# Row vectors of an attention kernel made by a VectorE block transpose and short transfers instead of TensorE transposes

## The chip, the cores and the metric

The kernel runs on one core of a Trainium2 chip. The metric is device time in microseconds (us) of one execution. Each time is the median of several executions, and the profile is one further execution with every instruction recorded. The engines are TensorE (PE), VectorE (DVE), ScalarE (ACT) and GpSimd (POOL); DMA transfers are issued from queues in order, here the queue of SyncE (SP) for nearly all, and POOL's for the loads of K, Q and V.

## The reference, cut to what matters

Two layers of a mixer trunk over 256 context tokens and 2048 latent tokens, width 1024, all in float32. Latent queries attend over all 2304 keys, context queries over the 256 context keys. The change touches only the softmax and the product of its result with a gate:

```python
def attend(q, k, v):                        # 8 heads, 96 wide, values 64 wide
    def one_block(qi):
        s = jnp.einsum('bqhd,bkhd->bhqk', qi, k).astype(jnp.float32) * sm_scale
        p = jax.nn.softmax(s, axis=-1).astype(v.dtype)
        return jnp.einsum('bhqk,bkhd->bqhd', p, v)
    ...
y_a = attn * jax.nn.silu(g_a)               # then two convolution branches y_b, y_c
y = jnp.concatenate([y_a, y_b, y_c], axis=-1)
x_new = x + gate[:, None, :] * (y @ w_out[l])
```

## The kernel before, in words

Activations are kept transposed, features on the partitions and tokens along the row. Products that need float32 accuracy are split into a rounded high part and a low rest and done as three matmuls (`mm3`, lines 194 to 196). Each layer has four phases, one after the other with some overlap: tokens (normalised input), features (the wide product with W_in, and the convolutions, whose vector work is the `cc` and `sgcl` lines), attention, project (the product with W_out). All instructions are emitted into a scheduler that lists them by priority, so the order on an engine follows from dependences, priorities and rotating buffers, not from a hand-written list.

**Attention.** A job is one head and one block of 512 queries: 32 jobs a layer, and in layer 0 eight more of 256 context queries, one for each head (these are grouped with the fourth block of their head). A job does two things.

- Max pass (`prepare`). For each 128 queries and each 512 keys, one matmul `pmax` (L985) and one VectorE reduction (L986), 20 of each for a job; only two PSUM buffers hold `pmax`. `finish` (L989) makes the negated maximum of every query, one column of 128 for each query tile. `turn` makes that column a row: up to four matmuls `pmt` (L994) against an identity, and one ScalarE copy (L995) into row 96 of the query tile Q. K has ones there, so that the score matmul subtracts the maximum by itself. The max pass of a later job runs `LEAD` pairs of key tiles ahead of the present one, at a raised priority.
- Key loop. For each of nine pairs of key tiles: six score matmuls (L1073 to 1075; the first reads 97 rows, the row of maxima among them), four ScalarE exponentials giving p and ph (L1076, 1077), one GpSimd subtraction pl = p - ph (L1078), two VectorE additions into the running sum `acc` in PSUM (L1083 for the first, L1085), and four matmuls into `po` with the values (L1100, 1101). `close` stores `o` to DRAM (`o_d`, L1108), transposes the sums (`psum_t`, L1113), adds them up and takes reciprocals into `rinv` (L1116), one number for each query and head.

**Project.** `prepare_y` builds blocks of y for 512 tokens. For the four attention blocks (k below 4, two heads each) it loads the two halves of the attention result (`yr`, `ylo`, from `o_d`, L1168 and 1169) and the gate (`yg`, L1170). It then spreads the reciprocals: for each of four token tiles a ScalarE copy to 64 columns for each head (`rr`, L1174) and a TensorE transpose into PSUM (`prr`, L1175). Three VectorE products follow: r + lo (L1176), times `prr` (L1177), times the gate (L1178). Blocks of y are prepared while the last jobs of attention still run. The output is stored from the SP queue (`out_xT`, L1202).

Of the kernel before, what the change touches and what calls it, by code (L numbers as in the profile page):

```python
# [9 lines left out]
F32 = mybir.dt.float32  # L10
F32R = mybir.dt.float32r
I32 = mybir.dt.int32
AF = mybir.ActivationFunctionType
ALU = mybir.AluOpType
AX = mybir.AxisListType
# [3 lines left out]
P = 128  # L19
# [4 lines left out]
NT = SEQ + CTX  # L24
NTT = NT // P
DEPTH = 2
H = 8
# [24 lines left out]
NE = 2  # L52
# [11 lines left out]
RR = 3  # L64
# [20 lines left out]
def trunk(ctx: ExitStack, tc: tile.TileContext, ins, out):  # L85
    nc = tc.nc
    V, S, G, PE = nc.vector, nc.scalar, nc.gpsimd, nc.tensor
# [4 lines left out]
    cst = pool(ctx, "cst")  # L92
    ps = pool(ctx, "ps", space=PSUM)
    dr = pool(ctx, "dr", space=DRAM)

    def psum(tag, name):
        return ps.tile([P, 512], F32, tag=tag, name=name, bufs={"a": 3, "b": 2}.get(tag, 1))
# [39 lines left out]
    gain = [cst.tile([P, KD, 2], F32, name=f"gain{l}") for l in range(DEPTH)]  # L137

    rcol = rinv[1][:, :, 0:1]
    mx = [cst.tile([P, 4, 97], F32R, name=f"mx{i}") for i in range(2)]  # L140
    zero = rinv[0].rearrange("p t h -> p (t h)")[:, :97]
    G.memset(zero, 0.0)
    for t in mx:
        for i in range(4):
            G.tensor_copy(t[:, i], zero)

# [8 lines left out]
    x1_d = dr.tile([D, NT], F32, name="x1_d")  # L157
    xs = [ins["xT"], x1_d]
    xg_d = dr.tile([D, NT], F32, name="xg_d")

    def rsqrt_steps(y, v, tmp, tmi):

# [30 lines left out]
    def mm3(out_, ahi, alo, bhi, blo, first, last):  # L193
        PE.matmul(out_, lhsT=ahi, rhs=bhi, start=first, stop=False)  # L194
        PE.matmul(out_, lhsT=ahi, rhs=blo, start=False, stop=False)  # L195
        PE.matmul(out_, lhsT=alo, rhs=bhi, start=False, stop=last)  # L196


    def halves(l, j, ws, hi, lo, by=None):
# [739 lines left out]
    def attention(l, start):  # L939
# [17 lines left out]
        count = [0]  # L957
# [12 lines left out]
        def prepare(h, s, n, k0):  # L970

            K, Vt, Q = kv[h]
            keys = [(a, min(512, NT - a)) for a in range(k0 * P, NT, 512)]
            m = mx[count[0] % 2]

            early = count[0] < NE
            count[0] += 1

            part = m
            nq = n // P  # L980
            steps = []

            def chunk(t, c, a, w):
                pm = psum("b", "pmax")
                PE.matmul(pm[:, :w], lhsT=Q[0:QK, s // P + t, 0], rhs=K[0:QK, a // P : (a + w) // P, 0], start=True, stop=True)  # L985
                V.tensor_reduce(part[:, t, c : c + 1], pm[:, :w], axis=AX.X, op=ALU.max)  # L986

            def finish():
                V.tensor_reduce(m[:, 0:nq, 96:97], part[:, 0:nq, 0 : len(keys)], axis=AX.X, op=ALU.max, negate=True)  # L989

            def turn():
                px = psum("b" if early else "e", "pmt")
                for t in range(nq):
                    PE.matmul(px[0:97, t * P : (t + 1) * P], lhsT=m[:, t, :], rhs=idr, start=True, stop=True)  # L994
                S.copy(Q[96:97, s // P : (s + n) // P, 0], px[96:97, :n].rearrange("p (a t) -> p a t", t=P))  # L995

            for t in range(nq):
                for c, (a, w) in enumerate(keys):
                    steps.append(lambda t=t, c=c, a=a, w=w: chunk(t, c, a, w))
            return steps, finish, turn  # L1000

        LEAD = 3
        queue = []
        sums = [0]

# [45 lines left out]
        for idx, job in enumerate(jobs):  # L1053
            h = job[0][0]
            if job[0][1] == (1024 if h else 512) and h + 1 < H:
                load(h + 1)
            pairs = [(j, it) for j in job for it in range(j[3], NTT, 2)]
            for pi, ((h, s, n, k0), kt0) in enumerate(pairs):
                if idx == len(jobs) - 1 and pi == len(pairs) - AE:
                    mark = tc.cur_priority  # L1060
                K, Vt, Q = kv[h]
                first, final = kt0 == k0, kt0 == NTT - 2
                if first:
                    po = psum("c", "po")
                    acc = psum("d", "acc")
                p = tp.tile([P, 2, 512], F32, tag="p", name="p", bufs=4)
                ph = tp.tile([P, 2, 512], F32R, tag="ph", name="ph", bufs=3)
                pl = tp.tile([P, 2, 512], F32R, tag="pl", name="pl", bufs=3)
                scs = []
                for z in range(2):  # L1070
                    kt, qt = kt0 + z, slice(s // P, (s + n) // P)
                    sc = psum("a", "sc")
                    PE.matmul(sc[:, :n], lhsT=K[0:97, kt, 0], rhs=Q[0:97, qt, 0], start=True, stop=False)  # L1073
                    PE.matmul(sc[:, :n], lhsT=K[0:QK, kt, 0], rhs=Q[0:QK, qt, 1], start=False, stop=False)  # L1074
                    PE.matmul(sc[:, :n], lhsT=K[0:QK, kt, 1], rhs=Q[0:QK, qt, 0], start=False, stop=True)  # L1075
                    S.activation(p[:, z, :n], sc[:, :n], AF.Exp, scale=scale)  # L1076
                    S.activation(ph[:, z, :n], sc[:, :n], AF.Exp, scale=scale)  # L1077
                G.tensor_tensor(pl[:, :, :n], p[:, :, :n], ph[:, :, :n].bitcast(F32), op=ALU.subtract)  # L1078
                flush()

                for z in range(2):
                    if first and z == 0:
                        V.tensor_copy(acc[:, :n], p[:, 0, :n])  # L1083
                    else:
                        V.tensor_tensor(acc[:, :n], acc[:, :n], p[:, z, :n], op=ALU.add)  # L1085
                for z in range(2):
                    at = pi + (z + 1) / 2 + LEAD
                    if at <= len(pairs):
                        ahead(idx + 1, at / len(pairs))
                    else:  # L1090
                        ahead(idx + 1, 1)
                        ahead(idx + 2, (at - len(pairs)) / len(pairs))
                if pi == len(pairs) // 2:
                    split_mods()
                if pi == len(pairs) - ME:
                    use_mods()

                def products(kt0=kt0, n=n, Vt=Vt, ph=ph, pl=pl, po=po, first=first, final=final):
                    for z in range(2):
                        PE.matmul(po[:, :n], lhsT=Vt[:, kt0 + z, :], rhs=ph[:, z, :n], start=first and z == 0, stop=False)  # L1100
                        PE.matmul(po[:, :n], lhsT=Vt[:, kt0 + z, :], rhs=pl[:, z, :n], start=False, stop=final and z == 1)  # L1101

                def close(h=h, s=s, n=n, po=po, acc=acc):
                    accs = op.tile([P, 512], F32, tag="o", name="accs", bufs=3)
                    S.activation(accs[:, :n], acc[:, :n], AF.Copy, scale=2.0)
                    o = op.tile([P, 512], F32, tag="o", name="o", bufs=3)
                    S.copy(o[:, :n], po[:, :n])
                    nc.sync.dma_start(o_d[l][h, :, s : s + n], o[:, :n])  # L1108

                    nq = n // P  # L1110
                    px = psum("e", "psum_t")
                    for t in range(nq):
                        PE.transpose(out=px[:, t * P : (t + 1) * P], in_=accs[:, t * P : (t + 1) * P], identity=idn)  # L1113
                    sm = tp.tile([P, 4], F32, tag="sm", name="sm", bufs=2)
                    V.tensor_reduce(sm[:, :nq], px[:, :n].rearrange("p (t k) -> p t k", k=P), axis=AX.X, op=ALU.add)
                    V.reciprocal(rinv[l][:, s // P : s // P + nq, h], sm[:, :nq])  # L1116

                late.append(products)
                if final:
                    late.append(close)  # L1120
# [10 lines left out]
    def project(l, start):  # L1131
# [22 lines left out]
        def prepare_y(bi):  # L1154
# [5 lines left out]
            for k in order:  # L1160
# [3 lines left out]
                else:  # L1164
# [3 lines left out]
                        nc.sync.dma_start(r[64 * z : 64 * z + 64, :n], o_d[l][2 * k + z, 0:64, s : s + n])  # L1168
                        nc.sync.dma_start(lo[64 * z : 64 * z + 64, :n], o_d[l][2 * k + z, 64:128, s : s + n])
                    nc.sync.dma_start(g[:, :n], sga_d[l][k * P : (k + 1) * P, s : s + n])  # L1170
                    px = psum("b" if bi == 0 else "cde"[k % 3], "prr")
                    for t in range(n // P):
                        rr = rp.tile([P, 2, 64], F32, tag="rr", name="rr", bufs=RR)
                        S.copy(rr, rinv[l][:, s // P + t, 2 * k : 2 * k + 2].unsqueeze(2).to_broadcast([P, 2, 64]))  # L1174
                        PE.transpose(out=px[:, t * P : (t + 1) * P], in_=rr.rearrange("p a b -> p (a b)"), identity=idn)  # L1175
                    V.tensor_tensor(r[:, :n], r[:, :n], lo[:, :n], op=ALU.add)  # L1176
                    V.tensor_tensor(r[:, :n], px[:, :n], r[:, :n], op=ALU.mult)  # L1177
                    V.tensor_tensor(r[:, :n], r[:, :n], g[:, :n], op=ALU.mult)  # L1178
                split(yh[:, k, :n], yl[:, k, :n], r[:, :n], V if bi == 0 and (SPV & 4 and k < 4 or SPV & 8 and k >= 4) else None)
                yield  # L1180

# [128 lines left out]
```

## Time and profile before

| what | us |
|---|---|
| median of 3 runs | 3695.61 (3680.32 to 3699.47) |
| the profiled execution's own time | 3695.0 |
| its span, from first to last instruction | 3693.2 |
| PE busy | 3529.8 (96%) |
| DVE busy | 2888.8 (78%) |
| POOL busy | 2341.6 (63%) |
| ACT busy | 2166.7 (59%) |

The mean granted clock of TensorE is 0.978 of full speed. Matmuls overlap in the trace: each is listed with the time from its start to its modelled end, while the next one may start earlier, so that what a matmul costs in a full row is the distance between starts. A profile group names the line, the engine, the output and the inputs of an operation.

### The profile page before, as it was taken

To read this page: it belongs to the slowest core of one execution; us is meant where nothing else is said; L and a number is where in the kernel's file an instruction comes from. 1 tells how busy PE (TensorE), PEld (TensorE's weight loads), DVE (VectorE), ACT (ScalarE), POOL (GpSimd) and SP (SyncE) were. 2 spreads that over 40 slices of the span, in tenths; PEclk is the share of its full clock that TensorE was granted. 3 is DMA by queue.
4 is the path that set the end of the run, shared out by engine and by line. 5 is a ranking of instruction groups with operands and counts; after the bars stand their busy time and mean duration, and the time that the engine had idled before them with its cause. 6 is when DMAs were issued, how large, how long until landed. Compare 5 with 4: busy or idle time off the path is not lost. (4 is left out here: it accounts for less than half of the span.)

```text
span 3693.2 us, 52810 instructions
## 1 busy us (share of the span) xinstructions
PE 3529.8 (96%) x17532; PEld 2916.9 (79%) x17532; DVE 2888.8 (78%) x5472; ACT 2166.7 (59%) x4328; POOL 2341.6 (63%) x1497
## 2 busy tenths in 40 slices
PE   7899999999999999999999989999999999998999
PEld 5787888887888787877788878887777777776777
DVE  5986977877888888888437878769988888888832
ACT  4665343247778777877445663433677777776720
POOL 4664344348888888877435654444687887877721
PEclk8999999999999999999999999999999999999999
DMA  7567333433333213312776773435232202222163
GB/s 219 171 186 205 82 107 110 113 112 78 79 79 88 61 45 82 85 58 64 232 231 207 215 213 100 114 99 125 80 76 61 41 27 61 59 61 75 43 197 114
DMA packets 394386, 411.47 MB, mean 111 GB/s; under 512 B 19168, under 2 KB 332128, under 8 KB 388960
## 3 DMA queue, kind: packets, MB, share of 16 engines
q1 hardware_dynamic: 387712, 333.87, 31.2%
q0 software_dynamic: 6400, 74.22, 8.9%
q8 instruction: 138, 2.26, 0.3%
q14 instruction: 136, 1.11, 0.1%
HBM read 266.72 MB, written 141.59 MB: 111 GB/s over the span
## 5 line engine op out<-in xcount | busy, mean ns | idle before, releaser
L1078 POOL TENSOR_TENSOR pl<-p,ph 128x1024 fp32r<-128x1024 f32 (+1 forms) x584 | 1387.2, 2397 | 276.2 <-ACT ph L1077 110.4
L986 DVE TENSOR_REDUCE mx<-pmax 128x1 fp32r<-128x512 f32 (+1 forms) x1296 | 795.1, 628 | 122.0 <-PE pmax L985 113.6
L1076 ACT ACTIVATE p<-sc 128x512 f32<-128x512 f32 x1168 | 713.4, 612 | 240.5 <-PE sc L1075 232.7
L1085 DVE TENSOR_TENSOR acc<-acc,p 128x512 f32<-128x512 f32 x1096 | 756.7, 690 | 55.9 <-ACT p L1076 29.5
L1077 ACT ACTIVATE ph<-sc 128x512 fp32r<-128x512 f32 x1168 | 703.8, 612 | 20.1 <-PE po L1100 16.2
L194 PE MATMUL pf<-hhf,wh 128*128 128x256 f32 (+1 forms) x1584 | 549.3, 348 | 18.2 <-ACT tg L867 8.4
L196 PE MATMUL pf<-hhf,wl 128*128 128x512 f32 (+1 forms) x1584 | 546.4, 347 | 4.5 <-POOL wl L191 3.7
L195 PE MATMUL pf<-hlf,wh 128*128 128x256 f32 (+1 forms) x1584 | 547.2, 346 | 0.0
L985 PE MATMUL pmax<-K,Q 96*128 96x512 f32 (+1 forms) x1296 | 465.0, 386 | 34.8 <-DVE mx L986 26.8
L1073 PE MATMUL sc<-Q,K 97*128 97x512 f32 x1168 | 476.5, 408 | 11.7 <-ACT ph L1077 9.3
L1101 PE MATMUL po<-pl,Vt 128*128 128x512 f32 x1168 | 467.9, 401 | 2.1 <-POOL pl L1078 1.8
L1074 PE MATMUL sc<-Q,K 96*128 96x512 f32 x1168 | 465.2, 398 | 0.0
L1100 PE MATMUL po<-ph,Vt 128*128 128x512 f32 x1168 | 461.9, 396 | 1.1 <-DMA Vt<-v_d 0.8
L1075 PE MATMUL sc<-Q,K 96*128 96x512 f32 x1168 | 462.4, 396 | 0.0
L191 POOL TENSOR_TENSOR wl<-wraw,wh 128x1024 fp32r<-128x1024 f32 x104 | 253.8, 2441 | 292.8 <-ACT wh L190 279.4
L747 DVE SCALAR_TENSOR_TENSOR cacc<-z,hv,cacc 128x384 f32<-128x384 f32 (+5 forms) x780 | 403.0, 561 | 14.3 <-ACT cacc L742 11.2
L194 PEld LDWEIGHTS pf<-hhf,wh 128*128 128x128 f32 x1584 | 303.7, 192 | 57.2 <-ACT wh L190 9.1
L196 PEld LDWEIGHTS pf<-hhf,wl 128*128 128x128 f32 x1584 | 303.0, 192 | 44.3 <-POOL wl L191 7.2
L985 PEld LDWEIGHTS pmax<-K,Q 96*128 96x128 f32 x1296 | 245.3, 190 | 116.9 <-DVE mx L986 58.6
L195 PEld LDWEIGHTS pf<-hlf,wh 128*128 128x128 f32 x1584 | 303.8, 192 | 36.1
L1073 PEld LDWEIGHTS sc<-Q,K 97*128 97x128 f32 x1168 | 222.2, 190 | 71.3 <-ACT ph L1077 20.0
L1075 PEld LDWEIGHTS sc<-Q,K 96*128 96x128 f32 x1168 | 224.5, 192 | 51.5
(257 smaller groups left out, 6189.0 us busy)
## 6 DMA issues: line engine op xcount, KB each, us to landing
wraw<-in_w_in SPq DMA_DIRECT2D x108, 512.0 KB
q_d<-sg SPq DMA_DIRECT2D x68, 384.0 KB
wm<-in_w_mod SPq DMA_DIRECT2D x46, 512.0 KB
v_d<-vs SPq DMA_DIRECT2D x36, 512.0 KB
kn_d<-sg SPq DMA_DIRECT2D x72, 256.0 KB
K<-kn_d POOLq DMA_DIRECT2D x16, 1152.0 KB, 8.5
Vt<-v_d POOLq DMA_DIRECT2D x16, 1152.0 KB, 14.8
o_d<-o SPq DMA_DIRECT2D x64, 256.0 KB
```

What stands on the lines that cost most here:

```text
L194: PE.matmul(out_, lhsT=ahi, rhs=bhi, start=first, stop=False)
L195: PE.matmul(out_, lhsT=ahi, rhs=blo, start=False, stop=False)
L196: PE.matmul(out_, lhsT=alo, rhs=bhi, start=False, stop=last)
L985: PE.matmul(pm[:, :w], lhsT=Q[0:QK, s // P + t, 0], rhs=K[0:QK, a // P : (a + w) // P, 0], start=True, stop=True)
L986: V.tensor_reduce(part[:, t, c : c + 1], pm[:, :w], axis=AX.X, op=ALU.max)
L1073: PE.matmul(sc[:, :n], lhsT=K[0:97, kt, 0], rhs=Q[0:97, qt, 0], start=True, stop=False)
L1075: PE.matmul(sc[:, :n], lhsT=K[0:QK, kt, 1], rhs=Q[0:QK, qt, 0], start=False, stop=True)
L1076: S.activation(p[:, z, :n], sc[:, :n], AF.Exp, scale=scale)
L1077: S.activation(ph[:, z, :n], sc[:, :n], AF.Exp, scale=scale)
L1078: G.tensor_tensor(pl[:, :, :n], p[:, :, :n], ph[:, :, :n].bitcast(F32), op=ALU.subtract)
L1085: V.tensor_tensor(acc[:, :n], acc[:, :n], p[:, z, :n], op=ALU.add)
L1101: PE.matmul(po[:, :n], lhsT=Vt[:, kt0 + z, :], rhs=pl[:, z, :n], start=False, stop=final and z == 1)
```

## The change

The maxima and the reciprocals take another way from columns to rows. `row_of` transposes a [128 x 32] tile by VectorE in blocks of 32 by 32 (`STREAM_TRANSPOSE`), so that each block of 32 partitions holds in its first rows 32 of the numbers of each query tile. Four transfers then write these pieces of 32 numbers (128 bytes) to a row in DRAM. For the maxima a fifth transfer reads the 512 numbers of the row into row 96 of Q. For the reciprocals, project reads rows of `r_d` back, spread over 64 partitions for each head, into a tile `rb`. The three VectorE products go through PSUM: r + lo is written to PSUM, the two others read it and one tile each. `LEAD` is 4 instead of 3, and eight GpSimd copies at the start become four memsets.

```diff
-    mx = [cst.tile([P, 4, 97], F32R, name=f"mx{i}") for i in range(2)]
-    zero = rinv[0].rearrange("p t h -> p (t h)")[:, :97]
-    G.memset(zero, 0.0)
-    for t in mx:
-        for i in range(4):
-            G.tensor_copy(t[:, i], zero)
+    mx = [(cst.tile([P, 4, 5], F32, name=f"mx{i}"), cst.tile([P, 32], F32, name=f"mn{i}")) for i in range(2)]
+    rs = [cst.tile([P, 32], F32, name=f"rs{i}") for i in range(2)]
+    for t in (mx[0][1], mx[1][1], *rs):
+        G.memset(t, 0.0)
...
+    m_d = [dr.tile([H, NT], F32, name=f"m_d{l}") for l in range(DEPTH)]
+    r_d = [dr.tile([H, NT], F32, name=f"r_d{l}") for l in range(DEPTH)]
...
+    def row_of(pl, dst, col, n):
+        t = pl.tile([P, 32], F32, tag="rowT", name="rowT", bufs=2)
+        V.transpose(out=t, in_=col)
+        nq = n // P
+        for b in range(4):
+            nc.sync.dma_start(dst.rearrange("(t p) -> t p", p=P)[:, 32 * b : 32 * b + 32], t[32 * b : 32 * b + nq, :])
...
             def turn():
-                px = psum("b" if early else "e", "pmt")
-                for t in range(nq):
-                    PE.matmul(px[0:97, t * P : (t + 1) * P], lhsT=m[:, t, :], rhs=idr, start=True, stop=True)
-                S.copy(Q[96:97, s // P : (s + n) // P, 0], px[96:97, :n].rearrange("p (a t) -> p a t", t=P))
+                row = m_d[l][h, s : s + n]
+                row_of(tp, row, m, n)
+                nc.sync.dma_start(Q[96:97, s // P : (s + n) // P, 0].bitcast(F32), row.rearrange("(o t p) -> o t p", o=1, p=P))
...
-        LEAD = 3
+        LEAD = 4
...
-                    V.reciprocal(rinv[l][:, s // P : s // P + nq, h], sm[:, :nq])
+                    ri = rs[s // 512 % 2]
+                    V.reciprocal(ri[:, :nq], sm[:, :nq])
+                    row_of(tp, r_d[l][h, s : s + n], ri, n)
...
-                    px = psum("b" if bi == 0 else "cde"[k % 3], "prr")
-                    for t in range(n // P):
-                        rr = rp.tile([P, 2, 64], F32, tag="rr", name="rr", bufs=RR)
-                        S.copy(rr, rinv[l][:, s // P + t, 2 * k : 2 * k + 2].unsqueeze(2).to_broadcast([P, 2, 64]))
-                        PE.transpose(out=px[:, t * P : (t + 1) * P], in_=rr.rearrange("p a b -> p (a b)"), identity=idn)
-                    V.tensor_tensor(r[:, :n], r[:, :n], lo[:, :n], op=ALU.add)
-                    V.tensor_tensor(r[:, :n], px[:, :n], r[:, :n], op=ALU.mult)
-                    V.tensor_tensor(r[:, :n], r[:, :n], g[:, :n], op=ALU.mult)
+                    rb = rp.tile([P, 512], F32, tag="rb", name="rb", bufs=2)
+                    for z in range(2):
+                        nc.sync.dma_start(rb[64 * z : 64 * z + 64, :n], r_d[l][2 * k + z : 2 * k + z + 1, s : s + n].to_broadcast([64, n]))
+                    px = psum("b" if bi == 0 else "cde"[k % 3], "py")
+                    V.tensor_tensor(px[:, :n], r[:, :n], lo[:, :n], op=ALU.add)
+                    V.tensor_tensor(px[:, :n], px[:, :n], rb[:, :n], op=ALU.mult)
+                    V.tensor_tensor(r[:, :n], px[:, :n], g[:, :n], op=ALU.mult)
```

Over the whole program TensorE loses 272 `pmt` and 136 `prr` matmuls, ScalarE 72 copies into Q and 136 copies `rr`; VectorE gains 144 block transposes, and the SP queue 720 transfers (288 to `m_d`, 288 to `r_d`, 72 into Q, 72 into `rb`). In the rows below, names such as `mx_90` are buffers of successive jobs, and lines after L139 have moved by up to ten in the changed kernel.

Because the scheduler lists by priority, the order of other work moves too. On DVE, where attention of layer 0 begins, the kernel before has the first copy of the running sum (`acc<-p`) between the last operations of the convolution branch (`sgcl`):

```order
L810 SCALAR_TENSOR_TENSOR sgcl<-ppw,hv,sgcl 128x392
L986 TENSOR_REDUCE mx_90<-pmax 128x1 x2
L1083 COPY acc<-p 128x512
L810 SCALAR_TENSOR_TENSOR sgcl<-ppw,hv,sgcl 128x392
L986 TENSOR_REDUCE mx_90<-pmax 128x1
L1085 TENSOR_TENSOR acc<-acc,p 128x512
```

At the same place of the changed kernel DVE has the first block transposes behind the last `sgcl`, and then the reductions of the next jobs:

```order
L820 SCALAR_TENSOR_TENSOR sgcl<-ppw,hv,sgcl 128x392
L992 TENSOR_REDUCE mx_91<-pmax 128x1 x2
L820 SCALAR_TENSOR_TENSOR sgcl<-ppw,hv,sgcl 128x392
L203 STREAM_TRANSPOSE rowT<-mn_90 128x32
L992 TENSOR_REDUCE mx_91<-pmax 128x1 x11
L995 TENSOR_REDUCE mn_92<-mx_91 128x4
L203 STREAM_TRANSPOSE rowT<-mn_92 128x32
L992 TENSOR_REDUCE mx_89<-pmax 128x1 x9
L227 COPY mrow<-pm 4x128 x2
L992 TENSOR_REDUCE mx_89<-pmax 128x1 x8
L1089 COPY acc<-p 128x512
```

So 28 reductions now stand between the first block transpose, which is behind the last `sgcl`, and the first copy of the sum; before, that copy stood ahead of the last `sgcl`.

On PE, at a change of job in layer 1, the kernel before has the four `pmt` matmuls between max matmuls of later jobs, and the next job's first score matmul (`sc`) three rows behind:

```order
L985 MATMUL pmax<-K,Q 128x512
L985 MATMUL pmax<-K,Q 128x256
L985 MATMUL pmax<-K,Q 128x512
L1101 MATMUL po<-pl,Vt 128x512
L1100 MATMUL po<-ph,Vt 128x512
L1101 MATMUL po<-pl,Vt 128x512
L985 MATMUL pmax<-K,Q 128x512
L994 MATMUL pmt<-idr,mx_90 97x128 x4
L985 MATMUL pmax<-K,Q 128x512 x2
L1073 MATMUL sc<-Q,K 128x512
```

The corresponding place of the changed kernel:

```order
L991 MATMUL pmax<-K,Q 128x256
L1119 MATMUL psum_t<-idr,accs 128x128 x4
L991 MATMUL pmax<-K,Q 128x512 x2
L1107 MATMUL po<-pl,Vt 128x512
L1106 MATMUL po<-ph,Vt 128x512
L1107 MATMUL po<-pl,Vt 128x512
L991 MATMUL pmax<-K,Q 128x512 x2
L991 MATMUL pmax<-K,Q 128x256
L991 MATMUL pmax<-K,Q 128x512 x4
L991 MATMUL pmax<-K,Q 128x256
L991 MATMUL pmax<-K,Q 128x512
L1079 MATMUL sc<-Q,K 128x512
```

The job's last max matmul is now at the top, several matmuls ahead of its first score matmul, and nine max matmuls of a later job stand in one run directly ahead of the score.

## Rows read from the trace of the kernel before

**Rows 1.** The page's first part: engine, busy us, share of span, instructions.
```profile
PE 3529.8 (96%) x17532; PEld 2916.9 (79%) x17532; DVE 2888.8 (78%) x5472; ACT 2166.7 (59%) x4328; POOL 2341.6 (63%) x1497
```
**Rows 2.** Windows: stretch, us, busy us by engine, PEclk, DMA share, GB/s.
```profile
core 0: us, PE busy (x) PEld busy (x) DVE busy (x) ACT busy (x) POOL busy (x), PEclk, DMA share, GB/s
1000.00:1100.00 100.00, 99.91 (x489) 80.75 (x489) 88.36 (x163) 80.26 (x152) 89.75 (x43) 1.00 0.31 73
2850.00:2950.00 100.00, 98.71 (x437) 78.19 (x436) 88.06 (x153) 75.48 (x144) 79.04 (x38) 1.00 0.15 31
...
1633.00:1643.00 10.00, 9.86 (x29) 7.37 (x29) 7.42 (x14) 4.45 (x8) 2.39 (x2) 0.64 0.24 69
```
**Rows 3.** Timeline of PE in layer 0: start, us, engine, line, operation.
```profile
1013.82 0.39 PE L985 MATMUL pmax<-K,Q 96*128 96x512 f32 x1
1014.05 0.48 PE L994 MATMUL pmt<-idr,mx 128*97 128x128 f32 x4
1014.37 0.45 PE L1101 MATMUL po<-pl,Vt 128*128 128x512 f32 x1
1014.65 0.39 PE L1100 MATMUL po<-ph,Vt 128*128 128x512 f32 x1
```
**Rows 4.** Instructions of tile pmt: count, ns least/median/most, first and last start.
```profile
L994 PE MATMUL pmt<-idr,mx x272: 221/248/368, 791.1 to 3472.0; 128*97 128x128 f32 x136
```
**Rows 5.** Tile prr, and PE's waits (us, times) for rr.
```profile
L1175 PE MATMUL prr<-idr,rr x136: 270/272/472, 1703.3 to 3644.1; 128*128 128x128 f32 x136
...
  ACT rr L1174: 8.4, 4
```
**Rows 6.** Timeline of PE in the first project phase.
```profile
1719.79 0.49 PE L1175 MATMUL prr<-idr,rr 128*128 128x128 f32 x3
1720.04 0.48 PE L1073 MATMUL sc<-Q,K 97*128 97x512 f32 x1
1720.36 0.39 PE L1074 MATMUL sc<-Q,K 96*128 96x512 f32 x1
```
**Rows 7.** Costliest groups: busy us, mean ns of one, idle before, releaser.
```profile
L986 DVE TENSOR_REDUCE mx<-pmax 128x1 fp32r<-128x512 f32 (+1 forms) x1296 | 795.1, 628 | 122.0 <-PE pmax L985 113.6
```
**Rows 8.** Timeline of all engines from the span's start; the bracket names a wait.
```profile
0.75 0.39 SPq L106 DMA_DIRECT2D rinv<-in_c  x1
...
1.19 0.41 SPq L110 DMA_DIRECT2D rinv<-in_idn  x1
...
2.56 1.28 ACT L124 ACT_TABLE_LOAD   x1 [2.56 <-DMA rinv<-in_c]
```
**Rows 9.** Chain of work that ended last, near the end: start, us, what.
```profile
3549.56 3.99 DMA out_xT<-xo
...
3559.06 3.22 DMA yr<-o_d
```
**Rows 10.** Timeline where attention of layer 0 begins.
```profile
812.48 0.39 PE L1073 MATMUL sc<-Q,K 97*128 97x512 f32 x1
...
817.37 0.68 DVE L1083 COPY acc<-p 128x512 f32<-128x512 f32 x1
...
817.96 0.62 DVE L810 SCALAR_TENSOR_TENSOR sgcl<-ppw,hv,sgcl 128x392 f32<-128x392 f32 x1
```
**Rows 11.** Timeline at a change of job in layer 1.
```profile
3048.16 0.17 DVE L989 TENSOR_REDUCE mx<-mx 128x4 fp32r<-128x20 f32 x1
...
3048.52 0.49 PE L994 MATMUL pmt<-idr,mx 128*97 128x128 f32 x4
3049.05 0.58 ACT L995 CAST Q<-pmt 1x512 fp32r<-1x512 f32 x1 [1.87 <-PE pmt L994]
...
3049.68 0.50 PE L1073 MATMUL sc<-Q,K 97*128 97x512 f32 x1
```
**Rows 12.** Timeline where the last job of layer 0 meets project.
```profile
1623.74 7.00 POOL L1078 TENSOR_TENSOR pl<-p,ph 128x1024 fp32r<-128x1024 f32 x3
...
1624.42 6.87 DVE L1176 TENSOR_TENSOR yr<-yr,ylo 128x512 f32<-128x512 f32 x1 [1.43 <-DMA yr<-o_d]
...
1632.54 0.80 PE L985 MATMUL pmax<-K,Q 96*128 96x512 f32 x1 [6.35 <-DVE mx L986]
```

## The prediction before the run

> **What bounds the kernel now.** I read the page's busy times first, then windows by stage, then the timelines at the places that the change touches. TensorE is busy 96% of the span, VectorE 78%, no other engine over 63% [rows 1]. A window inside attention of layer 0 has PE at 99.91 of 100 us, one in layer 1 at 98.71, VectorE at 88 in both [rows 2]. So time is won only by taking work off PE's row or waits out of it, and lost by any wait that puts a gap into a row that has none. The reader should look for two things: how far apart matmuls start (not how long each is), and how early the row of maxima is there before the first score matmul that reads it. ScalarE's and GpSimd's work taken away is worth nothing by itself.
>
> **What goes from PE.** In a full row four `pmt` matmuls start at 1014.05 and the next matmul at 1014.37, a step of 0.32; that one's successor comes 0.28 later instead of the usual 0.23 (1013.82 to 1014.05) [rows 3]. A group of four thus costs 0.37. There are 272 of them [rows 4]: 64 groups of four and 8 of two (taken as half, 0.19), 64 x 0.37 + 8 x 0.19 = 25.2 us. Three `prr` transposes cost 0.25 to the next start, and the matmul behind is 0.09 later than a step of 0.23 [rows 6]: 0.34 for three, 136 x 0.113 = 15.4 us. PE also waited 8.4 us for `rr` [rows 5]; this wait has no successor on PE. Together 49.0 us off.
>
> **What comes to other engines.** VectorE gets 144 block transposes. No row shows one; the nearest by its shape is the reduction of 128x20 numbers, 0.17 us [rows 11], so 24 us in all. VectorE has 12 us idle in 100 [rows 2], and a job gets only two of them: nothing, from 0 to 24 if they always stand in front of a reduction that PE waits for. SP gets 720 transfers at about 0.45 us of issue (0.75 to 1.19) [rows 8]. The transfer into Q waits on SP for four writes; behind it in that queue stand the stores of `o`, the loads of y and of W_out, which inside attention nobody needs for tens of microseconds. The lost copies of ScalarE and the start's GpSimd copies stood beside PE's work: nothing. The reciprocals' path to DRAM and back runs beside the store and reload of `o` itself, and such a store and load take 3.99 and 3.22 us [rows 9]: nothing on the path there.
>
> **The new wait: the row of maxima.** Before, the way was short: the negated maxima at 3048.16, `pmt` at 3048.52, the copy at 3049.05, the score at 3049.68 [rows 11]. Now it is: last max matmul 0.39 [rows 3], reduction 0.61 (795.1 over 1296) [rows 7], negation 0.17, transpose about 0.17, semaphores some 0.3, three issue steps 1.35 until the fourth write goes, a write, a load. A small load took from 0.75 to 2.56, 1.81 us [rows 8], twice 3.62. Sum 6.6, taken as 6.7. The upper bound puts 3.99 and 3.22 [rows 9] in place of the two 1.81: 10.3. The lower one, 5.4, has the four issues overlap wholly.
>
> What covers it is PE's work between the job's last max matmul and its first score matmul, by the order: 0.23 a matmul of 512 columns, and 0.61 for each max matmul beyond two in a run, since only two buffers hold them and the reduction's pace takes over. In layer 0 this is 13.7 us or more for all but one of the jobs, which has 9.1: enough. In layer 1 it repeats every eight jobs: 11.0, 16.3, 7.2, 6.3, 8.4, 6.5, 4.4, 5.3 (the place shown above, with its run of nine, is the 6.3). Against 6.7 these lack 0.4 + 0.2 + 2.3 + 1.4 = 4.3 in eight jobs; over the 32, whose first and last are better off, 12 us. At 5.4 it would be 3, at 8.7 46, at 10.3 some 79. I take 12, since the start's small load is nearest to these transfers in size; 128-byte pieces are in no row.
>
> The Trainium skill, in DMA: Bandwidth & Descriptors (Specifications), asks for 512 bytes or more in a transfer, since below that the DMA does a read-modify-write. No row here shows such a write. If it makes the write as long as the 3.99 of a whole store, the way is 8.9 and the sum would come out near 3725: the second rival below.
>
> **Max matmuls in runs.** In layer 1 the scheduler now lists longer runs of them: matmuls beyond the second of a run go from 24 to 52 by the order. Each waits 0.61 - 0.23 = 0.38: from 9 to 20 us, +11 (0 if VectorE has worked ahead).
>
> **The start of attention.** In layer 0 the first score went at 812.48 and the sum's first copy at 817.37, ahead of the last `sgcl` at 817.96 [rows 10]. Now 28 reductions stand between that `sgcl` and the copy: 0.62 + 28 x 0.61 = 17.7 after 817.96 is about 836, 18 later. PE has its own 28 max matmuls and 32 of modulation to do there, some 8 us, which leave the row elsewhere: +10 (0 to 18). Layer 1's start is reordered alike, with more feature work beside it: +2 (0 to 5).
>
> **The end of attention and project.** VectorE's product with two SBUF inputs stood 6.87 us beside GpSimd's subtractions, and PE waited 6.35 [rows 12]. After the change two of three products read PSUM and one tile; the first still reads two. I take -5 (-15 if all such waits go, +10 if the new loads come later than the old copies).
>
> The Trainium skill, in SBUF - State Buffer (Who interferes with whom), says that a VectorE instruction with two SBUF inputs contends with a GpSimd one that reads SBUF, and one with a single input does not. The 6.87 us row agrees. By the rule the third product can't be held any more, nor can a block transpose, which speaks against the third rival below.
>
> Against this the last jobs' rows for Q now queue on SP with the loads of W_out and y, where a load took 3.22 [rows 9], in jobs with 4.8 to 9.1 us of cover: +6 (0 to 15).
>
> **The clock.** After PE's wait of 6.35 us [rows 12] the granted clock was 0.64 in 1633 to 1643, against 1.00 inside attention [rows 2]: 3.6 us given away behind one such gap. The new gaps at the start of attention and in layer 1 are of 1 to 8 us: +5 (0 to 20).
>
> **Sum.** -25.2 - 15.4 - 8.4 + 10 + 2 + 12 + 11 + 5 - 5 + 6 = -8.0. The profiled execution took 3695.0 us, its span of 3693.2 and 1.8 around it; the sum gives 3687.0. The median of 3695.61 is 0.6 above it, and the three runs lie within 19 us.
>
> **Rivals.** First, the row is always in time: transfers of 2 KB land faster than 1.81, or real cover is longer since PE is held by other things anyway; the new max runs find VectorE ahead and no clock is lost. For it: LEAD 4 gives each max pass one pair more, and layer 0 has twice the cover needed. Against: 4.4 and 5.3 us in layer 1. Then -49 + 10 + 2 - 5 and nothing else, 3653.
>
> Second, the row is late: SP's queue, the write's completion and the read behind it take 8.7 us or more. Every second job of layer 1 then opens with a gap. For it: SP's own store and load of 3.99 and 3.22 [rows 9]. Against: those move 128 to 256 KB. At 8.7 the sum becomes 3687 - 12 + 46 = 3721; at 10.3, 3754. It is slower than before from 20 us of lack, a way of 7.3, and slower by over 0.5% (18 us, about what a measurement can tell from no change) from 38, a way of 8.3.
>
> Third, the block transposes are held by GpSimd's subtractions (7.00 us for three, 2.33 each) as the two-input product was [rows 12]: 144 by half of 2.33, 168 us on VectorE. Its idle 12 us in 100 cover the most, but reductions that PE waits for come later; a third on the path is 56, so 3743. Against: the reductions, which read one tile as the transposes do, take 0.61 us in the mean over the whole run [rows 7], so they are not held.
>
> **How the numbers follow.** The forecast 0.40, the first rival 0.34, the second 0.20, the third 0.06. So faster by over 0.5% 0.34, within 0.40, slower 0.26. The forecast's own range is 3670 to 3710. The range to hold eight times in ten goes below 3653 by the tail's -15 in place of -5, to 3642, and above up to between the second rival's 3721 and 3754, to 3740.
>
> **What would show it.** Right: `pmt` and `prr` gone, PE's busy time some 40 us less; before the first score of layer 1's jobs four or so short waits for a transfer into Q in eight jobs, 0.2 to 2.5 us each; none in layer 0; the first sum copy of layer 0 near 836; block transposes of 0.2 us. Wrong: waits for that transfer at nearly all jobs or 4 us long (second rival); none at all (first); block transposes of over 1 us (third); SP's transfers landing after 4 us; or a gain in PE's row well under 40 because VectorE, not PE, sets the pace of attention.

## The result and the profile after

The changed kernel is slower: 3779.14 us (median of 5 runs, 3775.43 to 3780.12) against 3695.61, a ratio of 1.023 with a 95% interval of 1.0208 to 1.0252. The forecast was 3687 in a range of 3642 to 3740.

The page's first part of the changed kernel, to be read against [rows 1]:

```profile
PE 3535.2 (94%) x17124; PEld 2903.0 (77%) x17124; DVE 2883.1 (76%) x5616; ACT 2095.6 (55%) x4120; POOL 2338.9 (62%) x1492
```

The span went from 3693.2 to 3778.1, 84.9 us more. PE has 408 instructions fewer, as counted, and yet 5.4 us more busy time; its idle time, span less busy, grew from 163.4 to 242.9, 79.5 us. So the matmuls are gone, but by their forecast price of 40.6 us those that are left took some 46 us more, and new gaps came on top.

Where the gaps are, the waits of PE say (engine, line, what for: us in all, times, longest). The changed kernel:

```profile
PE pmax L991 <- DVE mx L992: 39.4, 63, 4.0
PE sc L1079 <- DMA Q<-m_d: 33.7, 13, 10.4
...
PE pm L226 <- ACT wmh L192: 14.5, 1, 14.5
...
PE pmax L991 <- DVE mrow L227: 8.0, 2, 7.6
```

The kernel before:

```profile
PE pmax L985 <- DVE mx L986: 26.8, 37, 6.4
PE sc L1073 <- ACT Q L995: 1.5, 2, 1.4
```

The two others were not there. The windows (stretch, us, busy us of PE, PEld, DVE, ACT, POOL, PEclk, DMA share, GB/s) show the same, beside [rows 2]:

```profile
1000.00:1100.00 100.00, 99.89 (x480) 79.86 (x480) 86.06 (x170) 78.61 (x150) 89.44 (x42) 1.00 0.22 52
2850.00:2950.00 100.00, 89.34 (x364) 69.79 (x365) 76.01 (x135) 65.22 (x126) 70.68 (x33) 0.90 0.26 57
...
829.00:845.00 16.00, 1.49 (x3) 0.57 (x2) 2.21 (x4) 0.81 (x1) 0.00 (x0) 0.50 0.95 195
2893.00:2903.00 10.00, 9.55 (x32) 7.63 (x33) 6.05 (x10) 6.45 (x13) 4.93 (x3) 0.73 0.16 57
```

Layer 0 can be as full as before (99.89 of 100); the stretch in layer 1 has 89.34 where it had 98.71. At 829 to 845, the start of layer 0's attention, all engines nearly stand while the DMA engines are 95% busy. Behind PE's wait of 8.87 us that ends at 2893.45, shown below, the granted clock is 0.73 in the mean over 10 us, between its two levels of 0.50 (1.2 GHz; all of 829 to 845) and 1.00 (2.4 GHz; all of 1000 to 1100).

One late row in layer 1. The timeline shows, from POOL's queue, the loads of the next head's K and Q, and from SP's queue the four writes of a row and the load of it into Q:

```profile
2872.23 0.54 POOL L971 DMA_DIRECT2D K<-kn_d  x1
2872.66 1.26 SPq L206 DMA_DIRECT2D m_d<-rowT  x4
...
2873.29 0.52 POOL L975 DMA_DIRECT2D Q<-q_d  x1
...
2886.15 0.57 SPq L1001 DMA_DIRECT2D Q<-m_d  x1
...
2893.45 0.79 PE L1079 MATMUL sc<-Q,K 97*128 97x512 f32 x1 [8.87 <-DMA Q<-m_d]
...
2904.32 1.25 SPq L206 DMA_DIRECT2D m_d<-rowT  x4
2906.58 0.57 SPq L1001 DMA_DIRECT2D Q<-m_d  x1
```

The last write has been issued at 2873.92; the load, which waits for it, goes at 2886.15, 12.2 us later, and lands 7.3 us after that. The next row, with no load in flight, needs 1.0 us for the same (2905.57 to 2906.58); a row loaded in quiet at 3082.85 is there at 3084.68, after 1.83. The DMA view of 2868 to 2896 (bytes, us from issue to landing) says what was in flight:

```profile
Q<-q_d POOLq DMA_DIRECT2D x1, 1536.0 KB, 19.3
K<-kn_d POOLq DMA_DIRECT2D x1, 1152.0 KB, 8.4
Vt<-v_d POOLq DMA_DIRECT2D x1, 1152.0 KB, 15.1
K<-kr_d POOLq DMA_DIRECT2D x1, 594.0 KB, 13.0
```

These are 4.4 MB for a head, under way for some 23 us, and they begin when a finished head's buffers come free. Over the whole program the time between a row's last write and its load has a median of 1.01 us in 56 rows without such a load in flight (0.82 to 2.04), and reaches 20.17 in the 16 with one. A load in flight is not enough by itself: eight of the 16 rows took no more than 1.94. The three long ones inside layer 1 (11.5 to 12.8) were all written within 2 us of the first issue of a head's loads.

The second wait was foreseen by no rival. There are two row buffers, and in layer 0 the reciprocals of a head's fourth block and of its context block, 5 to 10 us apart, take both. VectorE's waits name it:

```profile
DVE rowT L203 <- DMA r_d<-rowT: 37.4, 6, 10.1
```

And the timeline shows one of the six:

```profile
977.48 0.20 DVE L203 STREAM_TRANSPOSE rowT<-rs 128x32 f32<-128x32 f32 x1
987.75 0.21 DVE L203 STREAM_TRANSPOSE rowT<-mn 128x32 f32<-128x32 f32 x1 [10.07 <-DMA r_d<-rowT]
...
988.79 0.80 PE L991 MATMUL pmax<-K,Q 96*128 96x512 f32 x1 [7.60 <-DVE mrow L227]
```

The transpose of the next maxima waits 10.07 us for an earlier row's write, again beside head loads; VectorE's other work stands behind it, and PE behind that. Third, the start of layer 0's attention:

```profile
844.19 1.04 ACT L192 CAST wmh<-wm 128x1024 fp32r<-128x1024 f32 x1 [30.63 <-DMA wm<-in_w_mod]
...
845.28 0.27 PE L226 MATMUL pm<-wmh,s 128*4 128x128 f32 x1 [14.51 <-ACT wmh L192]
```

PE's order now has 32 modulation matmuls ahead of the first score; their weights are loaded beside head 1's K and Q.

By the starts of score matmuls in both traces, the changed kernel is 32 us behind at the 147th, 56 at the last of layer 0, 66 at the first of layer 1, 85 at the last of layer 1 and 85 at the end.

### The profile page after: what moved, and what is told of

It reads as the page before. It is cut to its first block, busy times and chain, and to the rows that moved or that the text cites. A ratio compares the mean times of both kernels' runs of the same rounds, so it can differ in the third digit from the quotient of the medians.

```text
span 3778.1 us, 53150 instructions
## 1 busy us (share of the span) xinstructions
PE 3535.2 (94%) x17124; PEld 2903.0 (77%) x17124; DVE 2883.1 (76%) x5616; ACT 2095.6 (55%) x4120; POOL 2338.9 (62%) x1492
## 4 chain that ended last, share of the span: by engine, by line
PE 36%; DMA 7%; DVE 5%; issue 2%; ACT 1%; SPq 1%; POOL 1%; DVEq 0%; ACTq 0%; POOLq 0%
PE sc L1079 4%; PE sc L1080 4%; PE sc L1081 4%; PE po L1106 3%; PE po L1107 3%; PE pmax L991 3%; PE pf L196 3%; PE pf L198 3%; PE pf L197 3%; PE pout L196 2%; PE pout L197 2%; PE pout L198 2%; DMA m_d<-rowT 1%; DMA Q<-m_d 1%; DMA xk<-xg_d 1%
## 5 line engine op out<-in xcount | busy, mean ns | idle before, releaser
L992 DVE TENSOR_REDUCE mx<-pmax 128x1 f32<-128x512 f32 (+1 forms) x1296 | 794.4, 627 | 120.6 <-PE pmax L991 112.6
L1091 DVE TENSOR_TENSOR acc<-acc,p 128x512 f32<-128x512 f32 x1096 | 756.7, 690 | 79.2 <-ACT p L1082 54.8
L991 PE MATMUL pmax<-K,Q 96*128 96x512 f32 (+1 forms) x1296 | 492.1, 404 | 55.9 <-DVE mx L992 39.4
L1080 PE MATMUL sc<-Q,K 96*128 96x512 f32 x1168 | 472.1, 404 | 0.0
L1081 PE MATMUL sc<-Q,K 96*128 96x512 f32 x1168 | 469.0, 402 | 0.0
L991 PEld LDWEIGHTS pmax<-K,Q 96*128 96x128 f32 x1296 | 253.0, 196 | 157.5 <-DVE mx L992 93.2
```

## The experiments

Three theories stood against each other. **Head loads**: short transfers land late only while the next head is loaded. **SP's queue**: the 720 new issues hold up one another and others. **Order**: LEAD 4 and the new order of matmuls cost the time. Ratios are against runs of the kernel before, made on the same chip beside each experiment.

**1. Only the reciprocals new.** The kernel before, with

```diff
-                    V.reciprocal(rinv[l][:, s // P : s // P + nq, h], sm[:, :nq])
+                    ri = rs[s // 512 % 2]
+                    V.reciprocal(ri[:, :nq], sm[:, :nq])
+                    row_of(tp, r_d[l][h, s : s + n], ri, n)
```

and project as in the change.

> The kernel before with only the reciprocals taken the new way (block transpose, four short writes, rows read back in project); the maxima keep their TensorE transposes, LEAD stays 3. Theory of the head loads (short transfers issued while GpSimd's queue loads the next head's K, Q and V land after 5 to 20 us instead of about 1): nothing on PE's row waits for these transfers, and two row buffers are enough for one row per job, so the 15.4 + 8.4 us of the old way are won: about 3671 us (3660 to 3685). Rival of SP's queue (the new issues hold up the queue's other transfers): no gain, 3685 to 3700.

Measured: 3672.08 us, ratio 0.9944 (0.9921 to 0.9968). This half is a gain, 24 us, by the interval 12 to 29.

**2. Only the maxima new.** The changed kernel with `rinv`, `rr` and `prr` as before.

> The changed kernel with the reciprocals and project as in the kernel before; only the maxima go by short transfers, LEAD 4. Head loads: VectorE's holds for a row buffer go (one row per job, two buffers), the late rows at the start and at every eighth job of layer 1 stay, and the old project costs 24 us more: about 3765 us (3745 to 3785). If instead the order of the max pass (LEAD 4) alone costs the time, the same 3765; if the reciprocals' way is what costs, 3690 to 3710.

Measured: 3767.18, ratio 1.0194 (1.0173 to 1.0214). VectorE waits for no row buffer; PE waits 47.3 us for rows. The loss is in this half. Added up, the halves give 71 - 24 = 47 us, the whole change 83: the other 36 are what they do to each other. The two row buffers, which only the complete change fills up, are the first suspect.

**3. Eight row buffers.**

```diff
-        t = pl.tile([P, 32], F32, tag="rowT", name="rowT", bufs=2)
+        t = pl.tile([P, 32], F32, tag="rowT", name="rowT", bufs=8)
```

> The changed kernel with eight row buffers instead of two, so that no block transpose waits for an earlier row's write. Head loads: VectorE's waits for a row buffer (37 us, six times over 3 us) go, PE's waits for max reductions fall by about 20 us and the clock behind each comes back: about 3745 us (3735 to 3760). The late rows of layer 1 (9 to 10 us, three times) stay. If VectorE's holds were hidden or only moved, 3770 to 3780.

Measured: 3729.44, ratio 1.0082 (1.0055 to 1.0109): the kernel's loss falls from 2.3% to 0.8%, 50 us, more than the 30 expected, and two long waits for rows are left, of 8.6 and 9.1 us. VectorE's wait had been priced by PE's waits alone. From the 147th score matmul to the last of layer 0, where all six holds are, the changed kernel took 864.2 us at a clock of 0.97, this one 822.7 at 0.99 and the one with only the maxima new 823.9: 42 us are saved there. In layer 1, from first to last score matmul, it went from 921.1 to 909.7, with one long wait fewer.

**4. No loads of heads 2 to 7**, with the two buffers of the change.

```diff
         def load(h):
+            if h >= 2:
+                kv[h] = kv[h - 2]
+                return
```

> The changed kernel without the loads of K, Q and V of heads 2 to 7 in each layer: these heads use the tiles of heads 0 and 1 again, so that the attention of six heads is computed on other heads' data. All else is done as before. Head loads: the writes and loads of rows are then short everywhere but at each layer's start; VectorE's holds and layer 1's three long waits go, about 3725 us (3710 to 3740). SP's queue or the order as the cause: no change beyond 10 us, 3768 to 3780.

Measured: 3717.31, ratio 1.0064 (1.0039 to 1.0089). No transpose waits for a buffer though there are two, and layer 1's three long waits are gone; the longest for a row is 7.8 us, at the last job of layer 1. SP's queue still has all 720 transfers: their number is not the cause.

**5. Rows straight into Q**, eight buffers: four transfers from `rowT` to row 96 of Q, none through DRAM.

```diff
-                nc.sync.dma_start(Q[96:97, s // P : (s + n) // P, 0].bitcast(F32), row.rearrange("(o t p) -> o t p", o=1, p=P))
...
+                for b in range(4):
+                    nc.sync.dma_start(Q[96:97, s // P : (s + n) // P, 0, 32 * b : 32 * b + 32].bitcast(F32), t[32 * b : 32 * b + nq, :])
```

> The changed kernel with eight row buffers, and each row of maxima written by its four short transfers straight into row 96 of Q, with no row in DRAM and no fifth transfer. Head loads: one short transfer instead of two in a row is late while a head is loaded. Of the two long waits of layer 1 (8.6 and 9.1 us with eight buffers) some 2 to 5 are left, the short ones at other jobs (0.4 to 1.1) go, and the first score of layer 0 comes some 10 us earlier: about 3705 us (3690 to 3720) against 3729. If the order of the matmuls alone costs the time: 3722 to 3735.

Measured: 3755.5, ratio 1.0166 (1.0133 to 1.0199), slower than with the way through DRAM. A miss; PE's waits for the row:

```profile
PE sc L1079 <- DMA Q<-rowT: 58.1, 14, 9.3
```

Five heads of layer 1 now have a wait of 7.5 to 9.3 us, where two had one in experiment 3. The traces tell the reason: in these five the score goes 13.3 to 15.1 us after the row's last write was issued, against 19.7 and 20.4 in the two late rows of experiment 3. So the single transfer is less late than the two, but in the order that the scheduler made here five rows instead of two are written within 3 us of the start of a head's loads.

**6. No loads of heads 1 to 7**, eight buffers: the same edit with `h >= 1` and `kv[0]`.

> The changed kernel with eight row buffers and without the loads of K, Q and V of heads 1 to 7 in each layer: all heads use the tiles of head 0, so that seven heads are computed on head 0's data. Head loads: no wait for a row is left at the start of layer 0 either, which the run without heads 2 to 7 still had (15 us for the modulation weights behind head 1's load); with VectorE free of holds and layer 1 free of long waits about 3675 us (3655 to 3695). If the order or SP's queue costs the rest: 3705 to 3730.

Measured: 3670.83, ratio 0.9928 (0.9901 to 0.9954). Without loads in flight the late rows, the holds on VectorE and the wait for modulation weights are gone; PE waits 12.7 us for rows, 21 times: 4.4 at the start of layer 0, the other 20 at most 0.9 each, all in layer 1, where the cover is short. In layer 1's window the clock is full again:

```profile
2720.00:3400.00 680.00, 665.96 (x2902) 529.98 (x2901) 603.25 (x1092) 507.72 (x969) 544.00 (x231) 1.00 0.03 11
```

The same window of the changed kernel:

```profile
2720.00:3400.00 680.00, 637.71 (x2672) 500.00 (x2671) 558.58 (x999) 469.30 (x894) 516.83 (x237) 0.95 0.23 50
```

**7. LEAD alone**: the kernel before with LEAD 4.

> The kernel before with LEAD 4 instead of 3 and nothing else. Its runs of max matmuls in layer 1 stay as they were by the order. All transport theories: 3690 to 3702, no change. If the earlier max pass by itself costs time (as a rival has it for the changed kernel): 3705 to 3725.

Measured: 3694.88, ratio 1.0002 (0.9984 to 1.0021). In the kernel before, LEAD by itself costs nothing that shows.

**8. Experiment 1 with eight row buffers.**

> The kernel before with only the reciprocals taken the new way, as the first of the experiments, and eight row buffers instead of two. There is one row of reciprocals in some 27 us and two buffers were enough: no change against that run's 3672 us, 3662 to 3682.

Measured: 3673.07, ratio 0.9937 (0.9916 to 0.9958): no difference.

**9. Loads in shorter pieces**, eight buffers: each load of K, Q and V cut into four along its tiles (here K).

```diff
-            G.dma_start(K[0:NOPE], kn_d[l][h])
+            for u, v in cut:
+                G.dma_start(K[0:NOPE, u:v], kn_d[l][h, :, u:v])
```

> The changed kernel with eight row buffers and each load of K, Q and V cut into four, by key tiles or query tiles, so that a piece of one partition is 4.6 KB instead of 18 KB; bytes and queue are the same. If a short transfer waits behind the long pieces that the DMA engines hold at that moment, its wait falls from 14 to 16 us to some 4 and the long waits of layer 1 go: 3690 to 3720, with the longer runs of max matmuls that the scheduler makes of it taking part of the gain. If it waits for the whole loads, whatever their pieces: 3725 to 3750 against 3729.

Measured: 3802.78, ratio 1.0298 (1.0275 to 1.0321), the slowest of all and far from both expectations. The writes did become shorter. A row of layer 1 beside the loads:

```profile
3128.97 1.25 SPq L207 DMA_DIRECT2D m_d<-rowT  x4
...
3136.74 0.57 SPq L1007 DMA_DIRECT2D Q<-m_d  x1
...
3143.60 0.80 PE L1085 MATMUL sc<-Q,K 97*128 97x512 f32 x1 [9.87 <-DMA Q<-m_d]
```

Its write takes 6.5 us instead of 12.2; the worst behind the start of layer 0's attention is 7.6 instead of 12.8, though the load into Q still takes 6.9. But PE's waits for reductions rose to 58.3 us, with another order of the max matmuls, and its waits for rows to 54.8, one of 13.5 at the start of layer 0. So shorter pieces went with shorter writes; as the edit also changed the order of the loads and of the matmuls, their length alone is not singled out, and it is no cure here.

**10. Control: the kernel before without loads of heads 1 to 7.**

> A control: the kernel before without the loads of K, Q and V of heads 1 to 7 in each layer (seven heads are computed on head 0's data). The kernel before has no short transfer that PE waits for in attention, so head loads should cost it nothing: 3685 to 3700. If taking the loads away helps any kernel by itself, 3660 to 3680, and then the gain seen without loads in the changed kernel is not the rows' alone.

Measured: 3682.22, ratio 0.9966 (0.9953 to 0.9979). The loads cost the kernel before 12 us, more than expected. In the trace PE's waits for max reductions are 12.1 us instead of 26.8; why, is open. With eight buffers the loads cost the changed kernel 3729 - 3671 = 58.

**11. Maxima new in layer 0 alone**, LEAD 3, reciprocals new, eight buffers.

```diff
+            new = l == 0 and count[0] > NN
...
             def turn():
+                if new:
+                    row = m_d[l][h, s : s + n]
+                    row_of(tp, row, mm, n)
...
+                    return
                 px = psum("b" if early else "e", "pmt")
```

`count` already counts the present block and NN is 3, so that the new way begins with the fourth block, not with the fifth as the expectation has it: 37 rows.

> The reciprocals the new way in both layers with eight row buffers; the maxima the new way in layer 0 alone from its fifth block on, where 12 to 17 us of PE's work lie between the last max matmul and the first score; layer 1 and the first four blocks keep the TensorE transposes; LEAD 3. Some 36 groups of pmt go, 28 x 0.37 + 8 x 0.19 = 12 us, against 3672 with all maxima old: about 3661 us (3650 to 3670). If rows come late in layer 0 too: 3672 to 3690.

Measured: 3676.1, ratio 0.9948 (0.9928 to 0.9969): no gain over experiment 8, and outside the expected range. Six waits for rows are left (6.5 us in all, the longest 2.1). No write takes over 2.2 us once the last is issued, but at five of the six the first goes only 2.9 to 4.3 us after the row's transpose. Ahead of it in SP's queue stand the writes of a row of reciprocals, and ahead of these a store of `o` that, beside head loads, took the queue 10.9 to 12.1 us to issue:

```profile
1159.16 12.11 SPq L1134 DMA_DIRECT2D o_d<-o  x1
1171.37 3.31 SPq L211 DMA_DIRECT2D r_d<-rowT  x4
1174.95 3.50 SPq L211 DMA_DIRECT2D m_d<-rowT  x4
1180.62 0.58 SPq L1016 DMA_DIRECT2D Q<-m_d  x1
```

That row's transpose was at 1171.38. The kernel before has such stores too, six of 4.1 to 7.9 us, and nothing that PE waits for behind them; without head loads no store takes over 2 us.

**12. The complete change, its loads held back.** Eight buffers, and before each load of the next head a copy of one column of the present head's second row into the new tile, so that the load cannot go before that row has landed:

```diff
+            row = kv[h - 1][2][64:97, GT, 0, 0:1] if h else None
+            if h:
+                G.tensor_copy(K[64:97, 0, 0, 0:1], row)
+                G.tensor_copy(K[0:33, 0, 0, 0:1], row)
             G.dma_start(K[0:NOPE], kn_d[l][h])
```

> The changed kernel with eight row buffers, complete, but the loads of the next head's K, Q and V wait until the row of maxima of the present head's second block is in Q (four one-column GpSimd copies from that row into the new tiles, which the loads then overwrite). The loads of some 25 us so begin just behind a row's landing and are over before the next row is made; those of head 1 no longer meet the first rows or the modulation weights. Head loads: all long waits go and the time is that of the kernel without loads, 3671, and the 12 us that loads cost the kernel before too: about 3683 us (3668 to 3698) against 3729. If the waits have another cause or come back at another job: 3715 to 3740.

Measured: 3688.59, ratio 0.9968 (0.9954 to 0.9981). Nothing is left out here: the same bytes, begun some us later, take 41 us off experiment 3's time. Its loads begin behind a landed row. The timeline of SP's queue has the row, issued into Q:

```profile
3077.89 0.57 SPq L1010 DMA_DIRECT2D Q<-m_d  x1
```

and that of GpSimd the copy that waits for it and the first load; the next row's writes come at 3100.11, 20 us later:

```profile
3079.99 0.18 POOL L974 CAST K<-Q 33x1 fp32r<-33x1 f32 x1 [4.71 <-DMA Q<-m_d]
...
3080.71 0.56 POOL L977 DMA_DIRECT2D K<-kr_d  x1
```

What is left, in PE's waits:

```profile
PE sc L1088 <- DMA Q<-m_d: 29.5, 21, 5.5
```

The longest, 5.5, is in layer 1 at a place where a head's loads still began 1 us ahead of a row, whose write then took 16.1 us; the next, 4.9 and 3.8, are in the last jobs, and 3.6 stands behind a write of 5.2 beside loads. The other 17 are at most 1.7 each, 15 of them in layer 1, where the cover is short.

**13. Held loads and maxima new in layer 0 alone**; layer 1's maxima by TensorE, its loads as before.

> The new way where it has cover: reciprocals in both layers with eight row buffers, maxima by short transfers in layer 0 alone (all blocks, LEAD 4) with the next head's loads held until the present head's second row is there; layer 1's maxima by TensorE transposes, LEAD 3, loads as before. If layer 1's short cover (21 waits for a row, 29.5 us, and the clock behind them) is what keeps the complete kernel with held loads at 3689, this one gains layer 0's 14 us on the 3673 of the kernel with new reciprocals alone: about 3660 us (3650 to 3670). If the maxima's way gains nothing even where rows are in time: 3670 to 3690.

Measured: 3670.86, ratio 0.9949 (0.9934 to 0.9964), as experiment 8 within the intervals; the 12 us expected did not come. Two windows of layer 0 tell where:

```profile
900.00:1600.00 700.00, 696.34 (x3393) 563.81 (x3391) 623.61 (x1210) 541.31 (x1024) 626.95 (x309) 1.00 0.28 71
1600.00:1740.00 140.00, 126.99 (x548) 98.81 (x547) 118.01 (x185) 91.38 (x175) 95.68 (x42) 0.93 0.28 82
```

And those of experiment 8:

```profile
900.00:1600.00 700.00, 698.93 (x3454) 563.88 (x3453) 619.07 (x1167) 550.62 (x1037) 610.09 (x279) 1.00 0.29 70
1600.00:1740.00 140.00, 134.65 (x628) 106.35 (x627) 119.46 (x203) 102.89 (x198) 108.54 (x48) 0.98 0.29 87
```

Layer 0's row stays full either way, and its 1607th score matmul comes at 1624.1 instead of 1636.5: the 12 us are won there. Most of them are lost in the layer's last two blocks, where PE waits 5.16 us for a reduction and 4.08 for exponentials, at a clock of 0.93: at the last score matmul of layer 0 it is 3 us ahead (1721.5 against 1724.8), at the first of layer 1 one behind. So the best version is the reciprocals alone, and the maxima's way has no gain that these runs could keep.

## Why the prediction was wrong

**The step that failed** is "The new wait: the row of maxima", in its price and in its scope. It took 1.81 us for a write and for a load from the quiet start of the program, with 3.99 and 3.22 as the upper bound. In quiet that was high for the write, done 1.0 behind its last issue, and right for the load, 1.83. But beside the start of a head's loads, with pieces of 9 to 18 KB a partition, they take 12.2 and 7.3: so it is, within some us, at the start of attention and at three jobs of layer 1 that lie eight apart. The profile before had the rows for it, in its list of DMA issues (KB, us from issue to landing), and they were not set beside the transfers:

```profile
K<-kn_d POOLq DMA_DIRECT2D x16, 1152.0 KB, 8.5
Vt<-v_d POOLq DMA_DIRECT2D x16, 1152.0 KB, 14.8
```

The ten short waits of the 13 are 4.5 us together, below the 12 forecast; the three others are 29.2. The second rival named late rows as the way to slower, but as a general delay with gaps at every second job, at 3721 to 3754; it was one job in eight, with gaps of 9 to 10, and the start.

**VectorE "nothing"** failed too. A transpose does take 0.20 us (24 us were forecast for 144, 29 it is), but it waits for a buffer that an earlier row's write holds, and everything on VectorE stands behind it. The forecast named what stands behind the waiting instruction on SP and not on VectorE. Experiment 3 takes 50 of the 83 us away; where these holds are it is 42 us shorter.

**The start** was put at +10; the first copy of the sum came at 859.16 instead of 836, and by the 147th score matmul the kernel was 32 us behind. The 14.5 us for modulation weights are a load beside head 1's; with the loads held back (experiment 12) the 147th is at 900.6 instead of 929.0.

**The clock** was put at +5. PE's busy time instead of falling by 40.6 rose by 5.4, while the mean granted clock fell from 0.978 to 0.958. From the first to the last score matmul of layer 1, 3592 PE instructions take 864.5 us of busy time at a mean clock of 0.95; in experiment 6, without the long gaps, 3599 take 829.5 at 1.00. With the gaps away the mean over the whole span is 0.975.

**A wrong reading.** The 8.4 us that PE waited for `rr` [rows 5] count the same two waits twice, 3.9 on PE and 4.5 on its weight loads. PE's own list has them once:

```profile
PE prr L1175 <- ACT rr L1174: 3.9, 2, 2.8
```

The sum would have been 3691.5, and the reciprocals' part 19 instead of 24; that experiment 1 measured just 24 is in part luck, as its interval holds both. The lower bound of the range comes out at 3643 by its own terms, not 3642. Neither decides anything here.

**Right were** the direction and rough size of what the reciprocals give, the cover of layer 0, the short waits of layer 1 without loads (8.3 us in experiment 6, against 12), and the end: from the first to the last matmul of layer 1's project it is 187.0 us (3586.6 to 3773.6), before 188.2 (3500.4 to 3688.6). The first rival, 3653, supposed that rows in time give all 49: without the loads the change is 11 us ahead of its control (3670.83 against 3682.22), so most is lost elsewhere; where, is not worked out. The third rival fell: no block transpose took over 0.214 us.

On the rule weighed before, of transfers under 512 bytes (the Trainium skill, DMA: Bandwidth & Descriptors, Specifications): in quiet the writes of 128-byte pieces are done in about 1 us, so no price near 3.99 shows. Another rule of the same page of the Trainium skill, DMA: Bandwidth & Descriptors (Queues, rings and completion order), bears on what was found: a DMA engine takes turns between queues, a whole packet of descriptors at a time. By it a short transfer waits for the packet of long pieces ahead of it on its engine. The fall of a write from 12.2 to 6.5 us with pieces of a quarter agrees in direction; how long a packet is, no run here shows.

What stays open: how a DMA engine orders a short transfer against the loads, and why the loads cost the kernel before 12 us.

## What to carry to other kernels

Price a small transfer on the critical path by what is in flight at the moments at which it runs, not by a quiet one: look for the large loads in the same stretch first. Count the buffers of whatever a transfer reads from, since an in-order engine that refills them inherits the transfer's delay and passes it on to all that stands behind. Take only the half of a change whose way back is not waited for: here reciprocals, which are read a phase later, gain 24 us, and maxima, which the next matmul reads, lose 71.

## What the runs showed of the hardware

Four 128-byte-piece writes and a 2 KB load, 1.0 and 1.83 us in quiet, took up to 20.2 and 7.8 us beside loads of 0.6 to 1.7 MB on another queue; with K in pieces of 4.6 KB instead of 18 KB the writes behind the start of layer 0's attention took at most 7.6. A store of `o` beside such loads took SP's queue up to 12.5 us to issue, and what stood behind it in the queue went later (experiment 11). And one wait of 8.87 us was followed by 10 us at a mean granted clock of 0.73, so that a gap cost more than its length.
